# A list scheduler that is told of the port shared by VectorE and GpSimd, and other durations for five kinds of operation

## The chip, the cores and the metric

The kernel runs on one core of a Trainium2 chip. Its engines work side by side, each through its own queue in order: TensorE (PE in the profile) multiplies, VectorE (DVE) and ScalarE (ACT) do elementwise work, GpSimd (POOL) does elementwise work on SBUF alone, and SyncE (SP) issues the DMAs. An instruction waits for semaphores of other engines, and everything queued behind it on its engine waits too. The metric is the time in microseconds of one execution; the median of several is compared.

## The reference, cut to what matters

One decoder layer over 2048 tokens of width 1024, all in fp32:

```python
h = rmsnorm(x, norm1_g); p = h @ w_in            # 1024 -> 2560
a = pool_mixer(p[pool columns])                  # trailing means over 2, 4, 8, 16 tokens
b = diff_attention(q, k, v, lam)                 # 4 heads: (softmax(q1 k1) - lam softmax(q2 k2)) v, causal
c = stick_breaking_attention(q, k, v)            # 4 heads: sigmoid scores times a running product, causal
x = x + concat(a, b, c) @ w_out
h2 = rmsnorm(x, norm2_g)
x = x + (silu(h2 @ w_gate) * (h2 @ w_up)) @ w_down   # 1024 -> 2816 -> 1024
return rmsnorm(x, final_norm_g)
```

## The kernel before, in words

**Numbers.** Each fp32 operand of a large product is held as two parts, a high part (ScalarE, `split`, L415) and the remainder (VectorE, L416); a product is three matmuls (L474 to L476, L562 to L564, L914 to L916): high by high, high by low, low by high.

**Stages.** The tokens go in four tiles of 512. The input projection of a tile (`a1_tile`: RMSNorm, transposes L462, drains L465 and L467, products L474 to L476 and L562 to L564) stores q, k and v to DRAM. Attention takes a tile pair by pair. Four pairs are differential (`att_diff`): scores L648/L649 with a mask L651, maximum on DVE L717, exponential on ACT L720, softmax statistics of one column on DVE L729 to L757, a scaling on POOL L742, the mix of the two maps on DVE L763. Two pairs are stick-breaking (`att_sb`): sigmoids on ACT L796 and L798, a scan on DVE L806, a product on POOL L810. Both then transpose (L672), split (L415, L416) and multiply by v (L771 to L773, L816 and L817). The output projection (`out_proj`) reads the heads back (L412), scales them (L882/L883 on PE, L887 on DVE), and multiplies by w_out, L914 to L916. The projections of later and earlier tiles are the work that PE does between the attention steps.

The SwiGLU part (`mlp`) comes last. Each 2x2 block product is made of seven half-size products with sums and differences of blocks (Strassen's scheme). `gate_up` takes weight columns in 22 steps for each of two token halves (`s`): POOL forms the weight sums (`add`, L952), ACT and DVE split them, PE does seven products (L474 to L476), ACT copies a bank out (L1107), DVE adds banks (L1111), ACT applies the SiLU (L1114), DVE multiplies (L1117), POOL forms sums of the results (L952) and SP stores them (L1120). In the first half `head_out` also prepares the second half's operands: POOL subtractions L1061 on blocks read back with DMAs (L1055). `down` loads w_down, forms sums alternately on DVE and POOL (L952), splits, multiplies, and adds the banks into the result (DVE L1303); `finish` normalises and stores (ACT L437, root steps on DVE L423 to L431, L1286).

**What sets the order.** Nothing of this is ordered by hand. Every step is recorded as an `Op` with an engine, a duration in ns, a priority and the buffers that it reads and writes. `Plan.schedule` then plays the program: an engine that becomes free takes, of the steps whose inputs are there by the plan's clock, the one of smallest priority, and the engines' instructions are issued in the order of the planned starts. The order is fixed from then on; the chip follows it with semaphores. The durations come from small formulas (`act_ns`, `dve_ns`, `scan_ns`, `pool_ns`, `dma_ns`) and constants, and a hand-over costs the `LAG` of the engine. Buffers are slots of rings, and a step that needs a slot waits in the plan until one is free. The plan knows each engine as independent of the others:

```python
# Plan.schedule, before: a ready step c is taken when its buffers are there
o.start, o.end = t, t + o.ns
free[e] = o.end
```

Of the kernel before, what the change touches and what calls it, by code (L numbers as in the profile page):

```python
# [97 lines left out]
class Op:  # L98
    __slots__ = ("eng", "ns", "fn", "prio", "deps", "need", "bufs", "seq", "ready", "start", "end", "out", "plan")


class Plan:
# [4 lines left out]
    MORE = {"dma": 1080.0, "pe": 0.0}  # L107

# [6 lines left out]
    def op(self, eng, ns, fn, r=(), w=(), prio=0.0):  # L115
# [23 lines left out]
        o.deps, o.bufs, o.plan = {d for d in deps if d.plan is self}, bufs, self  # L139
        for b in bufs:  # L140
            b.users.append(o)
# [3 lines left out]
    def schedule(self):  # L145
# [31 lines left out]
        for o in self.ops:  # L177
            if o.need == 0:
                heapq.heappush(future[o.eng], (0.0, o.seq, o))
        wake = [(free[e], e) for e in self.ENGINES]  # L180
        heapq.heapify(wake)
        done = []
        while wake:
# [40 lines left out]
            free[e] = o.end  # L224
            heapq.heappush(wake, (o.end, e))
# [37 lines left out]
def scan_ns(n):  # L263
    return 2.11 * n + 70
# [6 lines left out]
def dma_ns(nbytes):  # L271
    return max(nbytes / 360.0, 450.0)
# [3 lines left out]
def hybrid_block_kernel(  # L276
# [19 lines left out]
    nc = tc.nc  # L296
# [122 lines left out]
    def rsqrt(pl, rg, v, vb, n, prio):  # L419
# [3 lines left out]
        pl.op("dve", 75, lambda: nc.vector.tensor_scalar(  # L423
            yt().bitcast(I32), v().bitcast(I32), 1, None, ALU.logical_shift_right), r=[vb], w=[y], prio=prio)
        pl.op("dve", 75, lambda: nc.vector.tensor_scalar(
            yt().bitcast(I32), yt().bitcast(I32), -1, 0x5F3759DF, ALU.mult, ALU.add), r=[], w=[y], prio=prio)
        for _ in range(3):
            pl.op("dve", 75, lambda: nc.vector.tensor_mul(zt(), yt(), yt()), r=[y], w=[z], prio=prio)
            pl.op("dve", 75, lambda: nc.vector.scalar_tensor_tensor(
                zt(), zt(), -0.5, v(), ALU.mult, ALU.mult), r=[vb], w=[z], prio=prio)  # L430
            pl.op("dve", 75, lambda: nc.vector.scalar_tensor_tensor(  # L431
# [269 lines left out]
    def att_diff(pl, rg, t, p, q, ks, vs, prio):  # L701
        pv = rg["pv"].new()
        nch = t + 1
        for qp in range(2):
            rows = []
            for qb in range(2):
# [41 lines left out]
                pl.op("dve", 190, lambda lc=lc, sm=sm: nc.vector.reciprocal(sm.t[:, 28:29], sm.t[:, lc[1]:lc[1] + 1]),  # L748
                      r=lk + [(sm, "L")], w=[(sm, "rho")], prio=prio("stat"))
                pl.op("dve", 70, lambda lc=lc, sm=sm: nc.vector.tensor_scalar(  # L750
                    sm.t[:, 28:29], sm.t[:, 28:29], sm.t[:, lc[0]:lc[0] + 1], neglam, ALU.mult, ALU.mult),
                    r=lk + [(sm, "L"), c_lam], w=[(sm, "rho")], prio=prio("stat"))
                if nch > 1:
                    pl.op("dve", 70, lambda sm=sm: nc.vector.tensor_scalar_mul(
                        sm.t[:, 32:32 + nch], sm.t[:, 20:20 + nch], sm.t[:, 28:29]),
                        r=[(sm, ("f", 1))], w=[(sm, "rho")], prio=prio("stat"))
                pl.op("dve", 70, lambda lc=lc, g=g, sm=sm: nc.vector.tensor_copy(  # L757
# [705 lines left out]
```

## Time and profile before

| | |
|---|---|
| time of three runs | 2685.91 us median (2684.29 to 2689.05) |
| the profiled execution's own time | 2685.21 us |
| its span, first to last instruction | 2683.3 us |
| PE busy | 2582.0 us, 96%, 13836 matmul records |
| DVE busy | 1768.1 us, 66% |
| ACT busy | 1323.8 us, 49% |
| POOL busy | 879.9 us, 33% |
| mean granted clock of TensorE | 0.982 of full speed |
| DMA | 436.41 MB, mean 163 GB/s |

Busy time is the union of the instructions' spans on an engine. A row of a timeline has a start, a length, the engine, line and operation, and in brackets the idle time of the engine ahead of it with what ended it. TensorE's clock has two levels, 1.00 (2.4 GHz) and 0.50 (1.2 GHz).

### The profile page before, as it was taken

Reading aid. Unit: us, or ns where it says so; the run is one execution under the profiler, and the core shown is the slowest. Engines: PE = TensorE matmul, PEld = TensorE weight load, DVE = VectorE, ACT = ScalarE, POOL = GpSimd, SP = SyncE. Lnnn points to the kernel's source line nnn. Section 1 sums busy time; section 2 is a strip of 40 time slices with the busy share of each in tenths; the row PEclk is TensorE's granted clock in tenths of the full one; section 3 lists DMA queues with packets and bytes.
Section 4 is the critical chain, followed back from the end, with each engine's and each line's share of the span. In section 5 each row is a group of like instructions: output and inputs, shape, how many; then the busy total and the mean of one; then the engine's idle time right before and its main releaser. Section 6 shows DMA issues by size and latency. Waiting matters only on the chain.

```text
span 2683.3 us, 39226 instructions
## 1 busy us (share of the span) xinstructions
PE 2582.0 (96%) x13836; PEld 2158.9 (80%) x13836; DVE 1768.1 (66%) x3127; ACT 1323.8 (49%) x2645; POOL 879.9 (33%) x890
## 2 busy tenths in 40 slices
PE   8989989999999999998899999999999999999998
PEld 6878778878888788878878887887888887888886
DVE  6376977779778888886554554475444447558557
ACT  4265666657767566664433533353333333445444
POOL 2001313222443133241024466544544444132041
PEclk9999999999999999988999999999999999999999
DMA  6776564566455845535632455253222338335333
GB/s 209 243 263 199 198 226 155 169 207 214 137 169 154 274 142 177 197 126 166 198 119 99 168 171 187 107 174 109 103 109 88 113 136 298 104 95 197 93 91 121
DMA packets 192709, 436.41 MB, mean 163 GB/s; under 512 B 21240, under 2 KB 58232, under 8 KB 192512
## 3 DMA queue, kind: packets, MB, share of 16 engines
q1 hardware_dynamic: 192512, 433.91, 48.7%
q8 instruction: 108, 1.77, 0.3%
q14 instruction: 89, 0.73, 0.1%
HBM read 313.77 MB, written 120.06 MB: 162 GB/s over the span
## 4 chain that ended last, share of the span: by engine, by line
PE 62%; DVE 9%; DMA 4%; ACT 3%; issue 2%; POOL 2%; SPq 0%; DVEq 0%; POOLq 0%; ACTq 0%
PE bank L476 15%; PE bank L474 15%; PE bank L475 15%; DVE d L416 3%; PE bank L672 3%; PE bank L648 2%; DVE d L806 2%; PE bank L649 2%; PE bank L915 2%; PE bank L914 2%; PE bank L916 2%; DMA d<-wo_d 1%; POOL d L952 1%; PE bank L817 1%; PE bank L816 1%
## 5 line engine op out<-in xcount | busy, mean ns | idle before, releaser
L474 PE MATMUL bank<-d 128*128 128x512 f32 x2296 | 916.2, 399 | 8.4 <-ACT d L415 4.2
L476 PE MATMUL bank<-d 128*128 128x512 f32 x2296 | 908.6, 396 | 6.7 <-DVE d L416 6.4
L416 DVE TENSOR_TENSOR d<-d 128x512 fp32r<-128x512 f32 (+1 forms) x668 | 608.8, 934 | 458.4 <-ACT d L415 231.7
L475 PE MATMUL bank<-d 128*128 128x512 f32 x2296 | 906.8, 395 | 3.4 <-DVE d L416 3.4
L952 POOL TENSOR_TENSOR d<-d 128x512 f32<-128x512 f32 x336 | 520.6, 1558 | 870.4 <-DVE d L416 610.2
L415 ACT CAST d<-d 128x512 fp32r<-128x512 f32 (+1 forms) x668 | 489.0, 762 | 611.4 <-PE bank L476 364.7
L476 PEld LDWEIGHTS bank<-d 128*128 128x128 f32 x2296 | 433.5, 189 | 111.5 <-DVE d L416 11.0
L474 PEld LDWEIGHTS bank<-d 128*128 128x128 f32 x2296 | 434.7, 189 | 106.6 <-ACT d L415 5.6
L475 PEld LDWEIGHTS bank<-d 128*128 128x128 f32 x2296 | 434.2, 189 | 100.8 <-DVE d L416 5.3
L416 DVE TENSOR_TENSOR d<-bank,d 128x512 fp32r<-128x512 f32 (+4 forms) x381 | 220.0, 604 | 113.6 <-ACT d L415 104.8
L810 POOL TENSOR_TENSOR d<-d 128x512 f32<-128x512 f32 (+3 forms) x160 | 164.4, 1028 | 390.2 <-DVE d L806 323.8
L415 ACT CAST d<-bank 128x512 fp32r<-128x512 f32 (+4 forms) x381 | 187.7, 527 | 184.7 <-PE bank L672 108.2
L720 ACT ACTIVATE d<-bank,d 128x512 f32<-128x512 f32 (+3 forms) x320 | 198.6, 626 | 107.1 <-DVE d L717 102.5
L742 POOL TENSOR_SCALAR d<-d 128x512 f32<-128x512 f32 (+3 forms) x144 | 102.8, 730 | 440.5 <-ACT d L732 394.6
L648 PE MATMUL bank<-d 128*128 128x512 f32 (+3 forms) x480 | 199.9, 417 | 28.8 <-ACT d L720 10.9
L1107 ACT COPY d<-bank 128x512 f32<-128x512 f32 x132 | 77.6, 588 | 257.1 <-PE bank L476 231.9
L717 DVE TENSOR_REDUCE d<-bank 128x1 f32<-128x512 f32 (+3 forms) x320 | 186.8, 602 | 25.1 <-PE bank L649 12.6
L1111 DVE TENSOR_TENSOR d<-bank,d 128x512 f32<-128x512 f32 x176 | 121.1, 688 | 124.6 <-PE bank L476 117.8
L806 DVE TENSOR_TENSOR_SCAN d<-d,bank 128x512 f32<-128x512 f32 (+3 forms) x160 | 174.4, 1091 | 33.3 <-ACT d L798 15.6
L649 PE MATMUL bank<-d 128*128 128x512 f32 (+3 forms) x480 | 176.7, 371 | 0.0
L672 PE MATMUL bank<-ident,d 128*128 128x128 f32 x1088 | 156.3, 276 | 6.5 <-DVE d L763 5.4
L914 PE MATMUL bank<-d 128*128 128x256 f32 x512 | 153.3, 299 | 3.9 <-DMA d<-wo_d 2.8
(134 smaller groups left out, 3563.4 us busy)
## 6 DMA issues: line engine op xcount, KB each, us to landing
d<-in_w_gu_dram SPq DMA_DIRECT2D x88, 512.0 KB, 3.5
d<-in_w_in_dram SPq DMA_DIRECT2D x80, 512.0 KB, 4.9
d<-v_d SPq DMA_DIRECT2D x60, 512.0 KB, 4.3
d<-k_d SPq DMA_DIRECT2D x60, 512.0 KB, 4.8
d<-wo_d SPq DMA_DIRECT2D x52, 512.0 KB, 5.3
d<-q_d SPq DMA_DIRECT2D x48, 512.0 KB, 4.5
g_d<-d SPq DMA_DIRECT2D x66, 256.0 KB, 2.1
d<-g_d SPq DMA_DIRECT2D x66, 256.0 KB, 2.7
```

The source lines that it names most:

```text
L415: pl.op("act", act_ns(n, psum), lambda: nc.scalar.copy(hi(), src()), r=r, w=[whi], prio=prio)
L416: pl.op("dve", dve_ns(n), lambda: nc.vector.tensor_sub(lo(), src(), f32(hi())), r=[*r, *after, whi], w=[wlo], prio=prio)
L474: nc.tensor.matmul(o, a_hi, b_hi, start=first, stop=False, **kw)
L475: nc.tensor.matmul(o, a_hi, b_lo, start=False, stop=False, **kw)
L476: nc.tensor.matmul(o, a_lo, b_hi, start=False, stop=last, **kw)
L648: nc.tensor.matmul(s.t[:, :n], qh.t[:, c0:c0 + P], kt.t[:, r, :n], start=True, stop=False)
L649: nc.tensor.matmul(s.t[:, :n], qh.t[:, c0 + 256:c0 + 256 + P], kt.t[:, r, :n], start=False, stop=j < t)
L672: nc.tensor.transpose(tp.t[:, c:c + P], rows[qb][kb // 4].t[:, (kb % 4) * P:(kb % 4 + 1) * P], ident)
L720: pl.op("act", act_ns(n, True, 2), lambda s=s, n=n, e=e, mc=mc, lc=lc, sm=sm: nc.scalar.activation(e.t[:, :n], s.t[:, :n], AF.Exp, bias=sm ...
L806: pl.op("dve", scan_ns(n), lambda iv=iv, n=n, w=w, s=s, prev=prev: nc.vector.tensor_tensor_scan(iv.t[:, n - 1::-1], w.t[:, n - 1::-1], s.t ...
L914: nc.tensor.matmul(o, m[:, 0, cs], wh.t[:, k % 4, :], start=k == 0, stop=False)
L952: pl.op(eng, ns, lambda: en.tensor_tensor(out(), a(), b(), op), r=r, w=w, prio=prio)
```

## The change

The planner's rules and numbers are changed; no instruction is added or removed, and the counts on each engine in the built program are the same. Four things:

1. **The port.** A step gets a mark `port` if it runs on POOL, or if it runs on DVE, touches no PSUM bank, and calls an operation with two tensor inputs. While a marked step of one of the two engines runs in the plan, a marked step of the other is put off until its end. Where both become free at the same instant, the plan looks at DVE first. The chip is told nothing of this: only the order that comes out is issued.
2. **Durations on DVE.** The scan 2.20 n + 65 ns instead of 2.11 n + 70; the steps of the reciprocal root 105 ns instead of 75; four steps of the softmax statistics 70, 185, 135 and 110 instead of 190, 70, 70 and 70.
3. **Transfers.** 330 bytes per ns instead of 360 (512 KB: 1589 ns instead of 1456).
4. `TWO` names operations by the function that the step's code calls: `tensor_sub`, `tensor_mul`, `tensor_add`, `tensor_tensor`, `scalar_tensor_tensor`; the scan, reductions, copies and `tensor_scalar` aren't marked.

```diff
+    PORT = {"dve": "pool", "pool": "dve"}
+    TWO = {"tensor_sub", "tensor_mul", "tensor_add", "tensor_tensor", "scalar_tensor_tensor"}
...
+        psum = any(isinstance(b.ring.slots[0], tuple) for b in bufs)
+        o.port = eng == "pool" or eng == "dve" and not psum and not self.TWO.isdisjoint(fn.__code__.co_names)
...
+        port = {e: -1e9 for e in self.PORT}
...
+                if c.port and port[self.PORT[e]] > t:
+                    heapq.heappush(fut, (port[self.PORT[e]], c.seq, c))
+                    continue
...
+            if o.port:
+                port[e] = o.end
...
 def scan_ns(n):
-    return 2.11 * n + 70
+    return 2.20 * n + 65
...
 def dma_ns(nbytes):
-    return max(nbytes / 360.0, 450.0)
+    return max(nbytes / 330.0, 450.0)
...
-        pl.op("dve", 75, lambda: nc.vector.tensor_scalar(
+        pl.op("dve", 105, lambda: nc.vector.tensor_scalar(
...
-                pl.op("dve", 190, lambda lc=lc, sm=sm: nc.vector.reciprocal(sm.t[:, 28:29], sm.t[:, lc[1]:lc[1] + 1]),
+                pl.op("dve", 70, lambda lc=lc, sm=sm: nc.vector.reciprocal(sm.t[:, 28:29], sm.t[:, lc[1]:lc[1] + 1]),
```

In the new file a line stands 11 further down (L952 is L963, L720 is L731). PE's own order is the same behind the last score block of attention (L648), to the end of the program, but for eight transposes (L1040) that moved behind the first twelve gate_up matmuls. Ahead of it, groups of projection matmuls changed places with attention steps. Three places where the order of other engines moved follow.

**Place 1, ACT, the first attention pair of the program** (about 140 us). L720 (new L731) is the exponential of a score block, and frees its bank; L415 (L426) splits an input weight that a DMA brings; L465 (L476) drains transposes of the next tile. Before:

```order
L720 ACTIVATE d<-bank_226,d 128x128
L415 CAST d<-d 128x1024
L465 ACTIVATE d<-bank_214,g_sb 128x512
L465 ACTIVATE d<-bank_210,g_sb 128x512
L720 ACTIVATE d<-bank_218,d 128x128
L720 ACTIVATE d<-bank_222,d 128x256
L720 ACTIVATE d<-bank_226,d 128x256
```

After:

```order
L731 ACTIVATE d<-bank_226,d 128x128
L731 ACTIVATE d<-bank_218,d 128x128
L476 ACTIVATE d<-bank_214,g_sb 128x512
L731 ACTIVATE d<-bank_222,d 128x256
L731 ACTIVATE d<-bank_226,d 128x256
L476 ACTIVATE d<-bank_210,g_sb 128x512
L476 ACTIVATE d<-bank_214,g_sb 128x512
L426 CAST d<-d 128x1024
```

The weight split and one drain moved from ahead of the second exponential to behind the fourth.

**Place 2, POOL, the second half's operands within gate_up** (about 1580 to 1640 us). L1061 (L1072) is an operand subtraction, L952 (L963) a weight sum or a sum of results. Before:

```order
L1061 TENSOR_TENSOR d<-d 128x256 x10
L952 TENSOR_TENSOR d<-d 128x512
L1061 TENSOR_TENSOR d<-d 128x256 x2
L952 TENSOR_TENSOR d<-d 128x512 x2
L1061 TENSOR_TENSOR d<-d 128x256
L952 TENSOR_TENSOR d<-d 128x512 x2
L1061 TENSOR_TENSOR d<-d 128x256
L952 TENSOR_TENSOR d<-d 128x512
L1061 TENSOR_TENSOR d<-d 128x256
L952 TENSOR_TENSOR d<-d 128x512
L1061 TENSOR_TENSOR d<-d 128x256 x5
L952 TENSOR_TENSOR d<-d 128x512
```

After:

```order
L1072 TENSOR_TENSOR d<-d 128x256 x8
L963 TENSOR_TENSOR d<-d 128x512
L1072 TENSOR_TENSOR d<-d 128x256 x2
L963 TENSOR_TENSOR d<-d 128x512 x5
L1072 TENSOR_TENSOR d<-d 128x256
L963 TENSOR_TENSOR d<-d 128x512
L1072 TENSOR_TENSOR d<-d 128x256 x5
L963 TENSOR_TENSOR d<-d 128x512 x5
L1072 TENSOR_TENSOR d<-d 128x256 x8
```

The four weight sums of a step now stand together with the sum of results, with no operand subtraction between them.

**Place 3, DVE, the first product of `down`** (about 2240 to 2277 us). L416 (L427) splits an operand of the running product, L952 (L963) forms a weight sum for the third product, L1303 (L1314) adds the first banks. Before:

```order
L416 TENSOR_TENSOR d<-d 128x512 x8
L952 TENSOR_TENSOR d<-d 128x512
L416 TENSOR_TENSOR d<-d 128x512 x2
L952 TENSOR_TENSOR d<-d 128x512
L416 TENSOR_TENSOR d<-d 128x512 x2
L952 TENSOR_TENSOR d<-d 128x512
L416 TENSOR_TENSOR d<-d 128x512 x2
L952 TENSOR_TENSOR d<-d 128x512 x2
L416 TENSOR_TENSOR d<-d 128x512 x2
L952 TENSOR_TENSOR d<-d 128x512
L416 TENSOR_TENSOR d<-d 128x512 x2
L952 TENSOR_TENSOR d<-d 128x512
```

After:

```order
L427 TENSOR_TENSOR d<-d 128x512 x10
L963 TENSOR_TENSOR d<-d 128x512
L427 TENSOR_TENSOR d<-d 128x512 x2
L963 TENSOR_TENSOR d<-d 128x512
L427 TENSOR_TENSOR d<-d 128x512 x2
L963 TENSOR_TENSOR d<-d 128x512
L427 TENSOR_TENSOR d<-d 128x512 x2
L963 TENSOR_TENSOR d<-d 128x512
L427 TENSOR_TENSOR d<-d 128x512 x2
L963 TENSOR_TENSOR d<-d 128x512
L1314 TENSOR_TENSOR d<-bank_238,d 128x512
```

Five weight sums stand ahead of the first bank addition instead of seven.

## Rows read from the trace of the kernel before

**Rows 1.** Stretches: length, busy us (instructions) by engine, granted clock, DMA share, GB/s
```profile
200.00:1240.00 1040.00, 998.79 (x6414) 862.39 (x6413) 841.82 (x1566) 679.51 (x1550) 310.70 (x488) 0.98 0.56 183
1240.00:1350.00 110.00, 94.94 (x728) 90.20 (x728) 60.19 (x133) 38.18 (x73) 6.23 (x4) 0.92 0.53 172
2300.00:2400.00 100.00, 100.00 (x432) 80.74 (x431) 57.27 (x90) 41.14 (x72) 36.12 (x22) 1.00 0.32 90
```
**Rows 2.** Timeline of DVE and POOL near 1800 us, and either alone elsewhere
```profile
1805.47 8.55 DVE L416 TENSOR_TENSOR d<-d 128x512 fp32r<-128x512 f32 x5
1802.90 14.46 POOL L952 TENSOR_TENSOR d<-d 128x512 f32<-128x512 f32 x8 [4.29 <-DVE d L416]
2271.29 1.28 DVE L416 TENSOR_TENSOR d<-d 128x512 fp32r<-128x512 f32 x2
1539.82 1.29 POOL L952 TENSOR_TENSOR d<-d 128x512 f32<-128x512 f32 x1
```
**Rows 3.** Groups by line and form: count, busy us, mean ns, idle before
```profile
L806 DVE TENSOR_TENSOR_SCAN d<-d,bank 128x512 f32<-128x512 f32 x112 | 142.0, 1268 | 21.7 <-ACT d L798 6.2 <-ACT d L796 4.5 <-POOL d L801 2.3
L748 DVE RECIPROCAL d<-d 128x1 f32<-128x1 f32 x64 | 9.9, 155 | 1.6 <-ACT d L720 0.9
L750 DVE TENSOR_SCALAR d<-d,neglam 128x1 f32<-128x1 f32 x64 | 17.1, 267 | 0.0
```
**Rows 4.** Timeline of PE and ACT near 140 us
```profile
144.59 0.44 PE L648 MATMUL bank<-d 128*128 128x384 f32 x1 [3.98 <-ACT d L720]
141.97 1.04 ACT L415 CAST d<-d 128x1024 fp32r<-128x1024 f32 x1 [2.56 <-DMA d<-in_w_in_dram]
142.92 1.26 ACT L465 ACTIVATE d<-bank,g_sb 128x512 fp32r<-128x512 f32 x2
144.07 0.37 ACT L720 ACTIVATE d<-bank,d 128x128 f32<-128x128 f32 x1
```
**Rows 5.** Stretches, same columns as group 1
```profile
145.33:148.75 3.42, 3.42 (x16) 2.48 (x16) 2.76 (x11) 0.83 (x4) 0.00 (x0) 0.50 0.81 228
1630.00:1637.00 7.00, 6.22 (x15) 4.87 (x16) 0.63 (x1) 1.42 (x4) 6.03 (x8) 0.51 0.94 299
1632.00:1636.00 4.00, 4.00 (x10) 3.10 (x10) 0.00 (x0) 0.00 (x0) 3.10 (x5) 0.50 0.94 288
1640.00:1644.00 4.00, 4.00 (x19) 3.25 (x18) 3.23 (x5) 1.76 (x3) 2.56 (x2) 1.00 0.93 269
```
**Rows 6.** Timeline of POOL, ACT and PE, 1618 to 1631 us
```profile
1622.36 0.74 POOL L1061 TENSOR_TENSOR d<-d 128x256 f32<-128x256 f32 x1 [2.60 <-DMA d<-h_d]
1625.44 1.29 POOL L952 TENSOR_TENSOR d<-d 128x512 f32<-128x512 f32 x1
1628.68 1.04 ACT L415 CAST d<-d 128x1024 fp32r<-128x1024 f32 x1 [8.61 <-POOL d L952]
1630.78 0.80 PE L474 MATMUL bank<-d 128*128 128x512 f32 x1 [3.05 <-ACT d L1107]
```
**Rows 7.** Timeline of DVE from 2257 us; who waited for whom on PE, 2250 to 2280
```profile
2257.42 1.36 DVE L952 TENSOR_TENSOR d<-d 128x512 f32<-128x512 f32 x1 [0.33 <-DMA d<-in_w_down_dram]
2266.08 3.48 DVE L952 TENSOR_TENSOR d<-d 128x512 f32<-128x512 f32 x2
...
PE bank L476 <- DVE d L416: 3.1, 3, 1.2
PE bank L475 <- DVE d L416: 2.3, 3, 1.2
```
**Rows 8.** Timeline of PE near 2661 us, 1816 us, 1258 us and 401 us
```profile
2662.64 0.50 PE L475 MATMUL bank<-d 128*128 128x512 f32 x1 [1.06 <-DVE d L416]
1816.28 0.79 PE L476 MATMUL bank<-d 128*128 128x512 f32 x1 [2.63 <-DVE d L416]
1258.22 0.79 PE L882 MATMUL bank<-d,sel 8*128 8x512 f32 x1 [7.52 <-DVE d L887]
401.24 0.45 PE L648 MATMUL bank<-d 128*128 128x128 f32 x1 [4.66 <-DMA d<-k_d]
```

More of the change, by code (lines that the diff above doesn't have):

```diff
@@ L98 @@
 class Op:
-    __slots__ = ("eng", "ns", "fn", "prio", "deps", "need", "bufs", "seq", "ready", "start", "end", "out", "plan")
+    __slots__ = ("eng", "ns", "fn", "prio", "deps", "need", "bufs", "seq", "ready", "start", "end", "out", "plan", "port")
 class Plan:
@@ L422, in rsqrt @@
         yt, zt = (lambda: y.t[:, :n]), (lambda: z.t[:, :n])
-        pl.op("dve", 75, lambda: nc.vector.tensor_scalar(
+        pl.op("dve", 105, lambda: nc.vector.tensor_scalar(
             yt().bitcast(I32), v().bitcast(I32), 1, None, ALU.logical_shift_right), r=[vb], w=[y], prio=prio)
-        pl.op("dve", 75, lambda: nc.vector.tensor_scalar(
+        pl.op("dve", 105, lambda: nc.vector.tensor_scalar(
             yt().bitcast(I32), yt().bitcast(I32), -1, 0x5F3759DF, ALU.mult, ALU.add), r=[], w=[y], prio=prio)
         for _ in range(3):
-            pl.op("dve", 75, lambda: nc.vector.tensor_mul(zt(), yt(), yt()), r=[y], w=[z], prio=prio)
-            pl.op("dve", 75, lambda: nc.vector.scalar_tensor_tensor(
+            pl.op("dve", 105, lambda: nc.vector.tensor_mul(zt(), yt(), yt()), r=[y], w=[z], prio=prio)
+            pl.op("dve", 105, lambda: nc.vector.scalar_tensor_tensor(
                 zt(), zt(), -0.5, v(), ALU.mult, ALU.mult), r=[vb], w=[z], prio=prio)
-            pl.op("dve", 75, lambda: nc.vector.scalar_tensor_tensor(
+            pl.op("dve", 105, lambda: nc.vector.scalar_tensor_tensor(
                 yt(), zt(), 1.5, yt(), ALU.add, ALU.mult), r=[z], w=[y], prio=prio)
@@ L747, in att_diff @@
                     lk.append((sm, "L"))
-                pl.op("dve", 190, lambda lc=lc, sm=sm: nc.vector.reciprocal(sm.t[:, 28:29], sm.t[:, lc[1]:lc[1] + 1]),
+                pl.op("dve", 70, lambda lc=lc, sm=sm: nc.vector.reciprocal(sm.t[:, 28:29], sm.t[:, lc[1]:lc[1] + 1]),
                       r=lk + [(sm, "L")], w=[(sm, "rho")], prio=prio("stat"))
-                pl.op("dve", 70, lambda lc=lc, sm=sm: nc.vector.tensor_scalar(
+                pl.op("dve", 185, lambda lc=lc, sm=sm: nc.vector.tensor_scalar(
                     sm.t[:, 28:29], sm.t[:, 28:29], sm.t[:, lc[0]:lc[0] + 1], neglam, ALU.mult, ALU.mult),
@@ L753, in att_diff @@
                 if nch > 1:
-                    pl.op("dve", 70, lambda sm=sm: nc.vector.tensor_scalar_mul(
+                    pl.op("dve", 135, lambda sm=sm: nc.vector.tensor_scalar_mul(
                         sm.t[:, 32:32 + nch], sm.t[:, 20:20 + nch], sm.t[:, 28:29]),
                         r=[(sm, ("f", 1))], w=[(sm, "rho")], prio=prio("stat"))
-                pl.op("dve", 70, lambda lc=lc, g=g, sm=sm: nc.vector.tensor_copy(
+                pl.op("dve", 110, lambda lc=lc, g=g, sm=sm: nc.vector.tensor_copy(
                     l1[t][:, g, p:p + 1], sm.t[:, lc[0]:lc[0] + 1]),
```

## The prediction

> **What bounds the kernel now.** I read the stretches first. In the SwiGLU part PE is the bound: a full stretch of 100 us holds 432 matmuls of 512 columns, 0.2315 us each, with no idle time at all [rows 1]. That can't become shorter by another order; only the few places where PE stands still there can. From 200 to 1240 us, attention with projections between its steps, PE's records cover 998.8 of 1040 us, so 41.2 us are idle, DVE's cover 841.8 (81%) [rows 1]. From 1240 to 1350 us PE has 15.1 us idle. So what an order can win is the sum of PE's stops, and I went through PE's waits in order of time, then looked on the engine that ended each for what stood ahead of the releasing instruction.
>
> A stop costs more than its gap, since the granted clock fell to 0.50 (1.2 GHz) behind the first two of the stops below, after idle PE. Its price is read at either level: 10 matmul records in 4 us at 0.50, 19 at 1.00 [rows 5], so a half-clock stretch loses 9/19 of its length. The 7 us window at a mean of 0.51 holds 2 x 0.49 x 7 = 6.9 us of it, worth 3.2 us; the 3.42 us one is worth 1.6 us.
>
> **What the change tells the planner, against the trace.** No instruction is added or removed, so the direct price is nothing; all of it is what order comes out. The port rule is what the rows show: near 1805 us five splits of DVE took 8.55 us, 1.71 us each, while POOL's eight sums took 14.46 us, 1.81 us each; apart, two splits took 1.28 us and one sum 1.29 us [rows 2]. They took turns. The scan's 1268 ns record is nearer to the new 1191 than to the old 1150, the reciprocal's 155 ns is nearer to 70 than 190, the step behind it at 267 ns nearer to 185 than 70 [rows 3]. The planner's clock comes closer to the chip's, and most where DVE and POOL share the port, in the SwiGLU part, and where an instruction waits for a transfer.
>
> **Place 1, 140 us.** PE stood 3.98 us for an exponential, L720. On ACT a weight split L415 had come first, which itself waited 2.56 us for its DMA, then two drains L465 of 1.26 us; the L720 ran at 144.07 [rows 4]. With transfers counted longer, the split stands behind the fourth exponential. The gap's 3.98 us and the clock's 1.6 us could go, 5.6 us in all. But the first drain now waits for one exponential more and the others for three, some 0.4 to 1.3 us by L720's 0.37 us and larger forms, and transposes need those banks. I take 4.0; the bounds are 0 (the split's wait for the DMA just stops the next exponentials) and 5.6.
>
> **Place 2, 1631 us.** PE stood 3.05 us for a bank copy L1107 of ACT. The copy stood behind a split L415 that had waited 8.61 us for POOL's sum L952, and that sum stood behind operand subtractions L1061, one of which idled POOL for 2.60 us on a DMA of h_d [rows 6]. The old plan slipped a subtraction between sums that depend on each other; the new one issues five sums in a row. A sum can't be held up by h_d in the middle of its step then. Gap and clock are 3.05 + 3.2 = 6.3 us. I take 6.0; the bounds are 0 (eight subtractions in a row stand ahead of the sums, and an idle wait in them holds up the sums as before) and 6.3. What is late next there is the bank addition on DVE, which waits for PE there and not for POOL, so I cost it at nothing.
>
> **Place 3, 2254 to 2277 us.** PE waited six times for splits, 3.1 + 2.3 = 5.4 us [rows 7], without a fall of the clock. DVE had seven sums L952 between the splits of the first product; with POOL's turns they took 1.36 us, or 3.48 us for two [rows 7]. Two of the seven move behind the first bank additions, where the second product has its splits early. At some 1.4 us each, that is 2.8 us. The bounds are 0 and 5.4.
>
> **Place 4, 2661 us.** PE stood 1.06 us for a split [rows 8] that came behind two of the last normalisations L1286 on DVE. In the new order the last of these splits stand ahead of both. I take 1.0. The tail behind the last matmul has the same links, so nothing more.
>
> **Place 5, against it, 1816 us.** PE stood 2.63 us for the end of the run of five splits in [rows 2, 8]. The new order has six splits of that form in the run, between the same multiplication L1117 and bank addition L1111. POOL's sums are still there. One more split at 1.71 us: +1.7, bounds 0 and 1.7.
>
> **Unchanged.** At 1258 us PE stood 7.52 us for a head that had to be scaled; the four loads of heads are queued on SP behind the same loads of x, and both orders are equal there. At 401 us it stood 4.66 us for a key tile that goes to DRAM and back [rows 8]; PE's transposes ahead of it stand in the same places. I cost both at nothing.
>
> **The rest of attention.** Counting columns ahead of each score block in both orders, at 0.2315 us per 512 columns, at most 9.3 us more projection work stands ahead of the same attention step, and at most 6.4 us less. The plan puts more filler where DVE and POOL are now counted slower. That can turn some of the 41.2 us idle into work, or delay the scores that DVE waits for. I take 0 with bounds of 9.3 us either way, since at no step does more change places. On SP, single loads and stores changed places with the next one there; their landing is part of the same bounds.
>
> The Trainium skill, in SBUF — State Buffer, section "Who interferes with whom", has a rule that bears on this: whichever of the two engines issues first keeps the shared pair for its whole instruction, and issue order decides who is held up. The turns in [rows 2] agree. By that rule a plan that looks at DVE first in a tie binds nobody on the chip, which is the second rival below.
>
> **The sum.** -4.0 - 6.0 - 2.8 - 1.0 + 1.7 + 0 = -12.1 us. Against the profiled execution's own 2685.2 us that is 2673.1; it lies 0.7 us under the median of the three runs, so I say 2673 us, 0.5% less.
>
> **The rivals.** *The stops only move* (no change): the port is shared as before whatever the plan thinks, so the places that hang on POOL's turns, 2 and 3, keep their stops, at other instructions. Left are places 1, 4 and 5: -4.0 - 1.0 + 1.7 = -3.3, so 2682 us; a band of 2680 to 2690 belongs to it. For it speaks that POOL's waits are bound to DVE's splits, whose number is the same; against it that place 2 hangs on a DMA that stands ahead of a sum, which the order does decide.
>
> *DVE starves in attention* (slower): the plan now holds POOL back whenever DVE has a marked step, so it plans the products L810 and scalings L742 later than they happen, and puts projection matmuls ahead of the next scores. DVE has then nothing to do where it is the busiest but PE, and at the end of the stage there is no filler left. The price is the 9.3 us shift, and one more half-clock stretch like the one at 1631 us (3.2 us) for each stop of 3 us; with two of these and place 5, and places 1 to 4 at half (6.9 us), that is 9.3 + 6.4 + 1.7 - 6.9 = +10.5, 2696 us. It decides from the point where PE's idle time between 200 and 1240 us grows by more than the 12 us of the forecast, to 53 us. Against it: DVE has 19% idle in that stretch, and the filler's total is the same.
>
> *Attention gains too*: the shift fills idle time, -9.3 - 12.1, so 2664 us.
>
> **How the numbers follow.** Forecast 2673 us (2667 to 2679): 0.44. Attention gains too: 0.16. Stops only move, 2680 to 2690: 0.24. DVE starves: 0.16. About 0.2%, 5.4 us, is what a measurement of this kernel can tell from no change. The first two give faster, 0.60; the third 0.24 no change; the last 0.16 slower. With all bounds in favour, -5.6 - 6.3 - 5.4 - 1.1 + 0 - 9.3, the time is 2657; the upper end has to take in part of the slower case. The range is 2657 to 2693 us.
>
> **What would show it.** Place 1: no gap of more than 1 us ahead of a score block near 140 us, and no 0.50 there. Place 2: no POOL idle time for h_d directly ahead of a sum that ACT waits for, and no half clock between 1620 and 1640 us. Place 3: PE's waits for L416 at the start of `down` under 3 us. Place 4: none near the end. Place 5: a stop of 2.6 to 4.5 us there. The port's turns should be as before, sums of POOL near 1.8 us beside DVE's splits [rows 2]. Idle PE in attention of more than 53 us would show the starving case; the prediction is wrong too if a new stop with a fall of the clock appears in the SwiGLU part, where the changed orders of ACT and DVE have places that I didn't go through.

## The result, and the profile after

The changed kernel takes 2653.26 us (median of four runs, 2647.58 to 2655.8) against 2687.16 (2684.29 to 2689.05) for the kernel before beside it: 0.9872 of the time, 95% interval 0.9852 to 0.9892, some 34 us less. The forecast was 2673 us, 12 us less, and the range began at 2657. The sign was right; the size was not. Each kernel's time is the median of its runs, without one run of f1 (6400.74 us) and one of the kernel before (4891.44 us) that stand far outside the others.

The changed file's lines are 11 further down: L415 is now L426, L416 L427, L720 L731, L887 L898, L952 L963, L1061 L1072. First the stretches of [rows 1] and the two parts into which everything below is divided: the **attention part**, up to PE's last product of the output projection, and the **SwiGLU part**, from there to the last matmul. In these rows come the stretch in us, its length, then busy time and number of records of PE, PEld, DVE, ACT and POOL, the mean granted clock, DMA share and GB/s. After:

```profile
200.00:1240.00 1040.00, 1005.64 (x6489) 876.92 (x6486) 843.48 (x1612) 686.17 (x1563) 310.87 (x488) 0.97 0.56 186
1240.00:1350.00 110.00, 95.10 (x678) 90.49 (x679) 55.10 (x103) 38.99 (x75) 6.32 (x4) 0.87 0.52 171
1350.00:2650.00 1300.00, 1288.55 (x5572) 1043.31 (x5570) 738.36 (x1135) 504.49 (x819) 540.82 (x364) 1.00 0.40 135
...
0.00:1339.00 1339.00, 1277.38 (x8237) 1118.19 (x8238) 1001.38 (x1976) 811.49 (x1810) 333.11 (x526) 0.96 0.58 192
1339.00:2641.00 1302.00, 1295.93 (x5600) 1049.06 (x5599) 739.70 (x1121) 511.13 (x834) 542.57 (x365) 1.00 0.41 136
```

And the attention part of the kernel before, as one stretch:

```profile
0.00:1349.00 1349.00, 1276.69 (x8233) 1107.08 (x8234) 1014.18 (x1977) 812.13 (x1811) 334.63 (x526) 0.97 0.58 190
```

The same 8235 or so matmuls end at 1339 us instead of 1349. By the end of PE's last record of L916 the attention part went from 1349.5 to 1339.0 us, **10.6 us less**; the SwiGLU part went from 1323.2 to 1302.3 us, **20.9 us less**; the tail behind the last matmul gave 1.2 back. The span is 30.3 us shorter in these two executions. In the SwiGLU part PE's order is the same in both but for the eight transposes at its start; PE has 6.1 us idle left of 18.5, and half clock (0.50, 1.2 GHz) for 6.8 us instead of 20.5.

PE's stops that answer to [rows 4, 6, 8], after (start, length, engine, line, operation, shapes, in brackets the idle time ahead and what ended it):

```profile
60.64 0.77 PE L485 MATMUL bank<-d,bdh 128*128 128x512 f32 x1 [3.80 <-DVE d L427]
152.39 0.79 PE L659 MATMUL bank<-d 128*128 128x512 f32 x1 [2.70 <-ACT d L731]
395.66 0.45 PE L659 MATMUL bank<-d 128*128 128x128 f32 x1 [1.26 <-DMA d<-k_d]
1244.42 0.79 PE L893 MATMUL bank<-d,sel 8*128 8x512 f32 x1 [7.03 <-DVE d L898]
1795.06 0.50 PE L485 MATMUL bank<-d 128*128 128x512 f32 x1 [1.40 <-ACT d L426]
```

The stop at 1631 us of [rows 6] is gone; the place is now at 1615 us. So is the one at 2661. The stop at 1816 us [rows 8] shrank from 2.63 us to 0.53, with the 1.40 ahead of it that the last row shows. Place 1 still stops, 2.70 us for an exponential where it was 3.98, and a stop of 3.80 us at 57 us is new; the same matmul had waited 0.53 us before:

```profile
57.54 0.47 PE L474 MATMUL bank<-d,bdh 128*128 128x512 f32 x1 [0.53 <-ACT d L415]
```

PE's SwiGLU instructions stand in one order in every kernel here, but for eight transposes L1040 at the start, which stand behind twelve gate_up matmuls in the change, f9, f10, f12 and g3. So the time at PE's n-th matmul can be compared directly. Between the end of the attention part and matmul 9019 the change gains 1.4 us, from there past place 2 (to 9460) 6.7, past place 5 (to 10356) 3.0, to 12086 0.8, through place 3 (to 12150) 7.0, to the end, with place 4, 2.0. That is the 20.9. The 3.0 of place 5 is a sum: the 240 matmuls around its stop give 2.8, a stop of 0.82 us for a bank copy at 1855 us that went gives 1.1, and the matmuls ahead, with a new stop of 0.35 us at 1755 us, take 0.7 back.

### The profile page after: what moved, and what is told of

Read it like the earlier page. It is cut to its first block, busy times and chain, and to the rows that moved or that the text cites. A ratio compares the mean times of both kernels' runs of the same rounds, so it can differ in the third digit from the quotient of the medians.

```text
span 2653.0 us, 39234 instructions
## 1 busy us (share of the span) xinstructions
PE 2573.6 (97%) x13836; PEld 2167.2 (82%) x13836; DVE 1749.4 (66%) x3127; ACT 1323.8 (50%) x2645; POOL 875.7 (33%) x890
## 4 chain that ended last, share of the span: by engine, by line
PE 82%; DVE 7%; DMA 5%; ACT 3%; issue 2%; SPq 0%; POOL 0%; DVEq 0%; ACTq 0%; POOLq 0%
PE bank L485 18%; PE bank L487 18%; PE bank L486 18%; PE bank L683 4%; PE bank L659 4%; PE bank L660 3%; DVE d L427 3%; PE bank L926 2%; PE bank L925 2%; PE bank L927 2%; PE bank L573 2%; PE bank L574 2%; PE bank L575 2%; PE bank L828 1%; PE bank L827 1%
## 5 line engine op out<-in xcount | busy, mean ns | idle before, releaser
L427 DVE TENSOR_TENSOR d<-d 128x512 fp32r<-128x512 f32 (+1 forms) x668 | 601.8, 923 | 434.9 <-ACT d L426 223.0
L963 POOL TENSOR_TENSOR d<-d 128x512 f32<-128x512 f32 x336 | 520.1, 1556 | 854.8 <-DVE d L427 629.5
L426 ACT CAST d<-d 128x512 fp32r<-128x512 f32 (+1 forms) x668 | 488.1, 762 | 543.5 <-PE bank L487 358.3
L427 DVE TENSOR_TENSOR d<-bank,d 128x512 fp32r<-128x512 f32 (+3 forms) x381 | 219.7, 605 | 124.4 <-ACT d L426 122.3
L426 ACT CAST d<-bank 128x512 fp32r<-128x512 f32 (+3 forms) x381 | 187.4, 528 | 196.5 <-PE bank L683 123.6
L731 ACT ACTIVATE d<-bank,d 128x512 f32<-128x512 f32 (+3 forms) x320 | 198.9, 626 | 97.5 <-DVE d L728 84.1
```

Of the source, the lines that this page charges most:

```text
L426: pl.op("act", act_ns(n, psum), lambda: nc.scalar.copy(hi(), src()), r=r, w=[whi], prio=prio)
L427: pl.op("dve", dve_ns(n), lambda: nc.vector.tensor_sub(lo(), src(), f32(hi())), r=[*r, *after, whi], w=[wlo], prio=prio)
L731: pl.op("act", act_ns(n, True, 2), lambda s=s, n=n, e=e, mc=mc, lc=lc, sm=sm: nc.scalar.activation(e.t[:, :n], s.t[:, :n], AF.Exp, bias=sm ...
L963: pl.op(eng, ns, lambda: en.tensor_tensor(out(), a(), b(), op), r=r, w=w, prio=prio)
```

## The experiments

Two parts, two questions. For the SwiGLU part: **theory A**, the port rule makes the gain, against **rival B**, the slower transfers do. For the attention part: **theory D**, a plan with truer numbers gains, against **theory S**, any other order lands by chance within some 10 us (later 25) of before. A **theory E**, on the stop of 7 us at the end of attention, comes up with f9 and is named in some expectations ahead of it: the stop comes when more products of the output projection are left behind the last score block than stand behind the request for the last heads.

### One part of the change at a time

f1 has only the port rule, f2 only the durations on DVE, f3 only the transfers:

```diff
 # f1, against the changed kernel: the old scan_ns, root steps, statistics and
-    return max(nbytes / 330.0, 450.0)
+    return max(nbytes / 360.0, 450.0)
 # f2: the old transfers and
-                if c.port and port[self.PORT[e]] > t:
+                if False and c.port and port[self.PORT[e]] > t:
 # f3: without the rule, with the old durations, 330 kept
```

> The kernel before with the port rule alone; all durations and the 360 bytes per ns as before. Parts of the gain of 30.3 us of span in the trace of after: 10.6 us up to the last matmul of the output projection (attention part), 20.9 us from there to the last matmul (SwiGLU part, where PE's order is the same in both). Theory A, the port rule makes the SwiGLU gain: here the SwiGLU part is 18 to 22 us shorter than before, POOL's five weight sums stand in a row and no half clock is left near 1630 us. Rival B, the slower transfers make it: here the SwiGLU part is within 6 us of before. For the attention part theory S (any other order falls by chance within some 10 us of before on either side) says anything from -12 to +10; theory D (it is the plan's truer port that gains) says -8 to -14 us. Total by A with D about 2655 us.

> The kernel before with the durations of scan, root steps and softmax statistics alone, no port rule, 360 bytes per ns. POOL's order in the SwiGLU part and DVE's at the start of the last product are word for word those of before, so theories A and B both say that the SwiGLU part is within 2 us of before and keeps its stops near 1631, 1816 and 2257 us. The attention part: theory S says anything from -12 to +10 us, and theory D that it stays within 4 us of before. Total 2676 to 2698 us by S, 2682 to 2691 by D.

> The kernel before with 330 instead of 360 bytes per ns alone. Rival B, the slower transfers make the SwiGLU gain: 15 to 22 us shorter from the last output projection matmul on. Theory A: 0 to 8 us shorter, since POOL's weight sums stand four in a row in one step and as before in the other, and the splits at 1816 us still meet a full run of POOL's sums. Attention part: theory S from -12 to +10 us; if the plan's transfers make the attention gain, -8 to -14 us and the stop for the key tile near 401 us (4.66 us before, 1.26 us after) is gone here.

(The labels are shortened to f1, f2 and so on.) Measured: f1 2647.0 us, ratio 0.9856 (0.9829 to 0.9882); f2 2663.31, 0.9924 (0.9902 to 0.9945); f3 2677.32, 0.9969 (0.9955 to 0.9982). SwiGLU part: f1 20.1 us shorter, f2 0.8, f3 2.2. Theory A stands and B falls. (f3's profiled execution is one of its slowest: its two parts give 3.4 us where the medians differ by 8.3, so some 5 us more may belong to either part; B wanted 15 in the SwiGLU part.) In f2, PE's stops of [rows 6, 8] are where they were, and so are the rows that cause them: POOL idle for h_d in the middle of the sums, five splits at 1.71 us. f2, timelines of PE, POOL and DVE:

```profile
1607.90 0.79 PE L485 MATMUL bank<-d 128*128 128x512 f32 x1 [3.19 <-ACT d L1118]
1792.39 0.80 PE L487 MATMUL bank<-d 128*128 128x512 f32 x1 [2.63 <-DVE d L427]
...
1599.49 0.74 POOL L1072 TENSOR_TENSOR d<-d 128x256 f32<-128x256 f32 x1 [2.88 <-DMA d<-h_d]
1606.41 2.49 POOL L963 TENSOR_TENSOR d<-d 128x512 f32<-128x512 f32 x2
...
1781.56 8.56 DVE L427 TENSOR_TENSOR d<-d 128x512 fp32r<-128x512 f32 x5
```

The attention part was the surprise: f1 23.3 us shorter, f2 22.2, f3 1.2. Theory D had f1 at 8 to 14 us shorter and f2 within 4 us of before, theory S both at 12 us shorter at most.

### The rule in the SwiGLU part alone

```diff
         o.port = eng == "pool" or eng == "dve" and not psum and ...
+        o.port = o.port and fn.__code__.co_firstlineno >= 961      # f4
+        o.port = o.port and self.marking                           # f5
...
+    plan.marking = True                                            # f5
     mlp(plan, rm, 6e6)
```

> The kernel before with the port rule, where only steps recorded in the SwiGLU part carry the mark. PE's whole order is that of before, and every engine's up to the end of attention. The attention part must then be within 2 us of before (a check on how far equal orders scatter). Theory A: the SwiGLU part is 12 to 21 us shorter, less than 20.9 only where POOL's order near 1631 us, which has three sums in a row here and not five, keeps that stop (6 us). Rival B: within 6 us of before. Total by A 2666 to 2675 us, by B 2680 to 2687.

> As f4_port_in_swiglu, but every step that is recorded for the SwiGLU part is marked, the splits on DVE too, which a helper outside that part records and which f4 therefore left without the mark. PE's order is that of before throughout; POOL's five sums in a row and DVE's order at the start of the last product are those of f1_port. Theory A (the rule acts in the SwiGLU part by itself, through the turns of sums and splits): attention part within 3 us of before, SwiGLU part 17 to 22 us shorter, total 2663 to 2670 us. Rival C (the gain of f1 there hangs on what attention leaves behind): SwiGLU part within 6 us of before, total 2680 to 2688.

f4 did not do what its text says. It marked by the line on which a step's code stands, and the splits are recorded by a helper above that line, so sums and multiplications were marked and splits were not. It measured 2686.01 us, ratio 0.9997 (0.9981 to 1.0012); SwiGLU part 3.0 us shorter. Read as what it is, it says that the rule is worth next to nothing in all unless it binds the splits: place 2 alone gave 5.0 us, and other stretches took part of that back. POOL still idles for h_d between the sums there, and PE still stops, for half as long:

```profile
1623.60 0.74 POOL L1073 TENSOR_TENSOR d<-d 128x256 f32<-128x256 f32 x1 [2.63 <-DMA d<-h_d]
1624.30 1.29 POOL L964 TENSOR_TENSOR d<-d 128x512 f32<-128x512 f32 x1
...
1630.65 0.50 PE L486 MATMUL bank<-d 128*128 128x512 f32 x1 [1.46 <-ACT d L1119]
```

f5 marks the splits too: 2670.93 us, 0.9942 (0.9927 to 0.9956). Attention part 2.4 us longer, with PE's order that of before; SwiGLU part 17.2 us shorter. So the rule acts there by itself, and rival C falls. f5, timelines of POOL near place 2 and place 5 and of DVE at place 5 (lines are one further in f4 and f5):

```profile
1615.63 1.29 POOL L964 TENSOR_TENSOR d<-d 128x512 f32<-128x512 f32 x1
1618.47 6.33 POOL L964 TENSOR_TENSOR d<-d 128x512 f32<-128x512 f32 x4 [1.55 <-DVE d L428]
1624.75 6.95 POOL L1073 TENSOR_TENSOR d<-d 128x256 f32<-128x256 f32 x8
...
1802.72 10.91 POOL L964 TENSOR_TENSOR d<-d 128x512 f32<-128x512 f32 x7 [3.56 <-DMA g_d<-d]
...
1800.77 9.21 DVE L428 TENSOR_TENSOR d<-d 128x1024 fp32r<-128x1024 f32 x7
```

And what PE waited for from 2230 to 2275 us, around place 3 (us in total, times, longest):

```profile
PE bank L488 <- DVE d L428: 1.2, 1, 1.2
PE bank L487 <- DVE d L428: 0.7, 1, 0.7
```

The five sums come without a subtraction between them, and eight subtractions follow. What each place gave, in us against before, from the times of the same matmuls:

| | place 2 | place 5 | place 3 | SwiGLU part |
|---|---|---|---|---|
| change | -6.7 | -3.0 | -7.0 | -20.9 |
| f1, rule | -6.8 | -6.1 | -5.4 | -20.1 |
| f5, rule here alone | -6.8 | -6.0 | -3.9 | -17.2 |
| f4, splits unmarked | -5.0 | +1.7 | -0.6 | -3.0 |
| f2, durations | -1.3 | -0.1 | 0.0 | -0.8 |
| f3, 330 | -2.3 | +1.0 | -2.3 | -2.2 |

### Direction or chance: the attention part

```diff
 # f6, away from the trace (f11: 2.11 n + 75 and nothing else)
-    return 2.11 * n + 70
+    return 2.02 * n + 75
-        pl.op("dve", 75, lambda: nc.vector.tensor_mul(zt(), yt(), yt()), ...
+        pl.op("dve", 45, lambda: nc.vector.tensor_mul(zt(), yt(), yt()), ...
 # f12, further towards it: 2.35 n + 65, root steps 170
```

> The kernel before with the scan and the root steps moved as far from the trace as the change moved them towards it: scan 2.02 n + 75 instead of 2.11 n + 70, root steps 45 instead of 75 ns; no port rule. It moves about as many PE instructions as f2_numbers did. Theory D (durations nearer to the trace give the 22 us that f2 gained in the attention part): here the attention part is at least 3 us longer than before. Theory S (the order of before is an unlucky draw, and another order of any cause gains or loses by chance): anything from -25 to +10 us. SwiGLU part within 3 us of before by both.

> The kernel before with one number moved by 5 ns: scan 2.11 n + 75 instead of + 70. 400 of PE's instructions change places, all in attention. It shows how far an order without a direction scatters. Theory S: the attention part moves by 5 us or more either way. Theory D (the direction of the durations matters): within 4 us of before. SwiGLU part within 2 us by both; 243 products left after the last score block, so the stop of 7 us stays by E.

> The kernel before with the scan and root steps moved further in the direction of f2, to what the trace of before shows: scan 2.35 n + 65 (1268 ns at 512 columns), root steps 170 ns; softmax statistics as in the change. No port rule, 360 bytes per ns. Theory D: the attention part is 22 to 32 us shorter than before, at least as much as in f2. Theory S: anywhere from -25 to +10 us. If f2 gained because its plan happened to end attention well (E alone), no more than the stop's 8 to 12 us is gained: 220 products are left after the last score block, as 218 in f2. SwiGLU part within 3 us of before.

f6: 2685.38 us, ratio 1.0 (0.999 to 1.001), attention part 1.3 us shorter. f11: 2686.99, 1.0005 (0.9995 to 1.0014), 2.6 us longer. f12: 2687.5, 1.0006 (0.9989 to 1.0023), 7.0 us shorter, and its SwiGLU part 10.4 us longer; root steps counted at 170 ns change DVE's order there too. Theory D as I had put it falls with f12: numbers nearer to single records of the trace gave a third of f2's gain there and nothing in all. But f6 lost time on the way (its last score block comes 22.6 us later than before) and got it back behind that, where it has less work left and no stop of 7 us. And f11, with 400 of PE's instructions moved, stays within 3 us. So S, any order good for 10 us either way, isn't what these show either.

### The parts in company

f7 is the change with 360, f8 without the rule, f10 with the old durations.

> The changed kernel with the old 360 bytes per ns: port rule and all durations. f1 (port) gained 23.3 us in the attention part, f2 (durations) 22.2, f3 (330) 1.2, all three together 10.6. If the parts have each a gain of their own and 330 loses 10 us or more in company (theory D), the attention part is 25 us or more shorter than before here, total under 2640. By S it lies anywhere between -25 and +10 with no tie to the sum of the two. SwiGLU part 18 to 22 us shorter by theory A.

> The changed kernel without the port rule: durations and 330 bytes per ns. By D with a 330 that costs nothing by itself (f3) the attention part is 20 to 24 us shorter; by D with a 330 that spoils the others 5 to 12 us; by S anywhere from -25 to +10. SwiGLU part within 5 us of before by theory A, total 2660 to 2690.

> The changed kernel with the old durations: port rule and 330 bytes per ns. 247 products are left after the last score block here, as in the changed kernel, against 197 with the port rule alone. Theory E: the stop of some 7 us with its half clock is back, and the attention part gains 10 to 16 us on before, 8 to 12 us less than f1's 23.3. If 330 adds nothing in company, as in f8 against f2, and the stop has another cause: 21 to 25 us. SwiGLU part 17 to 22 us shorter by theory A. Total 2650 to 2657 by E, 2640 to 2645 otherwise.

f7: 2658.88 us, 0.9901 (0.9887 to 0.9916), attention 10.5 us shorter, SwiGLU 18.4. f8: 2656.21, 0.9891 (0.9876 to 0.9906), 22.4 and 4.6. f10: 2663.9, 0.9918 (0.9901 to 0.9935), 7.9 and 14.4. The SwiGLU part is 14.4 us or more shorter wherever the rule binds the splits, and at most 4.6 us shorter where it doesn't. The attention gains do not add up: the rule 23, the durations 22, both together 10.5. That doesn't hang on one execution: the medians, less the SwiGLU part, give some 18 and 24 us for the rule (f1, g2), 22 for the durations and 9 for both. So D, with 25 us or more for f7, missed there; f8 fell below its range of totals, and f10 missed what E had for it (10 to 16 us of attention, 2650 to 2657 us) and what A had for its SwiGLU part (17 to 22).

### The stop of 7 us at the end of attention

Before and changed kernel have 244 and 247 output products of PE behind the last score block, and 205 behind the request for the last tile's heads, counted in the program's order; f1 has 197 and 202, so attention steps still run beside the request, and its stop is 1.22 us. f9 requests the heads one quarter earlier:

```diff
-AHEAD = 2
+AHEAD = 1
```

> The changed kernel with AHEAD 1 instead of 2: the heads of the last tile are requested one quarter of the output projection of tile 2 earlier. Only 79 of PE's 13974 instructions change places, all around the end of attention; 236 products of the output projection stand behind the request instead of 205, with 247 behind the last score block in both. Theory E: the 7 us stop near 1237 us and the half-clock stretch of 13.7 us at it come from the chain request, load, scaling, split, which has neither score blocks nor products to cover it when more products than those behind the request are left after the last score block (before and after: 244 and 247 against 205; f1: 197 against 202). Then the stop falls under 2 us here and the attention part is 7 to 13 us shorter than in the changed kernel, total 2640 to 2647 us. Rival F: the head loads wait on SP behind a load of x that waits for a store; then the stop stays over 5 us and the time within 3 us of 2653.

2652.04 us, 0.9877 (0.9858 to 0.9896): the same as the change. The stop did go, and two others stand where PE now meets the last attention pair without cover:

```profile
1227.28 1.87 PE L702 MATMUL bank<-ones_c,d 128*128 128x2 f32 x8 [2.49 <-ACT d L696]
1230.97 0.79 PE L893 MATMUL bank<-d,sel 8*128 8x512 f32 x1 [1.83 <-DVE d L898]
```

F is out, since the stop moved with the request and not with SP's queue; E named its cause and overrated its price. f10, with 247 products left, has the stop back at 6.88 us, as E said, though not the total.

### Again, and put together

g2 is f1, g3 the change, a second time on one chip; g1 has the durations everywhere and the rule in the SwiGLU part alone.

> The durations of the change everywhere, the port rule for steps recorded for the SwiGLU part alone (splits too), 360 bytes per ns. PE's order is that of f2_numbers to the last instruction, POOL's order in the SwiGLU part that of f1_port. If the two parts are separate: attention part 19 to 25 us shorter as in f2, SwiGLU part 15 to 21 us shorter as in f5, total 2643 to 2652 us, 35 us or more under before. If what one part gains is given back in the other: over 2655 us.

> f1_port a second time. If the attention part's 23 us belong to the order: 19 to 27 us again. If they were the scatter of one execution: nearer to 10. The total 3 to 10 us under the changed kernel in the first case, within 3 us in the second.

> The changed kernel a second time, on the chip of g1 and g2. If its attention part's 10.6 us belong to the order (with the stop of 7 us near 1237 us): 7 to 14 us shorter than before again, and the total 3 to 10 us over g2; if they were scatter: anything up to 20 us.

g1: 2649.02 us, 0.9848 (0.9831 to 0.9865); g2: 2646.4, 0.9842 (0.9823 to 0.9861); g3: 2655.15, 0.9872 (0.9855 to 0.9889). In g1 the attention part is 21.4 us shorter (f2: 22.2) and the SwiGLU part 18.6 (f5: 17.2): the two parts are separate and add up. g3 repeats the change: 14.8 and 19.1. g2's profiled execution, at 2653.55 us the slowest of its four, has only 11.9 in attention where f1 had 23.3, with one program; f1's profiled execution was its fastest. Rows of f1 and of g2 over the attention part:

```profile
0.00:1326.00 1326.00, 1268.19 (x8236) 1107.91 (x8236) 1004.47 (x1977) 809.88 (x1810) 335.81 (x526) 0.98 0.60 194
...
0.00:1337.00 1337.00, 1276.15 (x8233) 1116.21 (x8234) 1003.60 (x1977) 810.04 (x1810) 335.10 (x526) 0.97 0.58 192
```

Idle PE time hardly differs, 57.8 and 60.9 us; PE is busy 8 us longer with the same matmuls, at half clock for 78.5 us instead of 58.0. So one execution's attention part is good to some 10 us. By that part g2 speaks for scatter, by its total for the order; the medians say more: the rule alone stands 6 and 9 us under the change in the two studies. Their intervals overlap, so I don't call it faster, only not slower.

g1 and f7 differ in one thing, whether the rule binds the attention part too: 0.9848 (0.9831 to 0.9865) without, 0.9901 (0.9887 to 0.9916) with it, 21.4 against 10.5 us of attention. With the old durations the rule gains there (f1 against f5); with the new ones it loses some 11 us.

## Why the prediction missed, point by point

**What bounds the kernel** was read rightly: the time moved by PE's stops and the half clock behind them. In the SwiGLU part the idle time fell by 12.4 us, and 13.7 us less at half clock are worth 6.5 by the prediction's 9/19, 18.9 of the 20.9. In the attention part the idle time fell by 10.7 us and PE's busy time stayed.

**The steps that failed** are three terms of the sum. The rest of attention was put at nothing and gave 13.8 us; place 5 had the wrong sign, 4.7 us off; place 3 was charged for two sums alone, 4.2 us short. A stop that no term had, at 57 us, took 4.8 back. From the two profiled executions (us):

| term | taken | measured |
|---|---|---|
| place 1 | -4.0 | -1.5 |
| new stop at 57 us | none | +4.8 |
| rest of attention, with 401 and 1258 us | 0 | -13.8 |
| place 2 | -6.0 | -6.7 |
| place 5, its stretch | +1.7 | -3.0 |
| place 3 | -2.8 | -7.0 |
| place 4, its stretch | -1.0 | -2.0 |
| other SwiGLU stretches | 0 | -2.2 |
| tail | 0 | +1.2 |
| sum | -12.1 | -30.3 |

**Place 1** (-4.0, bounds 0 and -5.6): mis-sized. From the first score block, the same matmul of PE in every kernel, the tile's transposes take 16.8 us before and 15.2 after. It is the transfers' number that moved them: 14.6 to 15.2 us in the six kernels with 330 (the change, f3, f8, f9, f10, g3), 16.0 to 18.4 in all others. But most of the stop stayed, and 3.4 us of half clock with it. The lower bound had named why: the split's wait for its DMA stops the next exponentials. ACT, after:

```profile
149.57 1.04 ACT L426 CAST d<-d 128x1024 fp32r<-128x1024 f32 x1 [1.37 <-DMA d<-in_w_in_dram]
150.52 1.26 ACT L476 ACTIVATE d<-bank,g_sb 128x512 fp32r<-128x512 f32 x2
151.67 0.58 ACT L731 ACTIVATE d<-bank,d 128x384 f32<-128x384 f32 x1
```

The same three links stand there as in [rows 4], four exponentials further on.

**The stop at 57 us** (no term): the rule lets wide weight splits on DVE come ahead of the one that PE waits for. 3.80 us of idle time and 6.8 us of half clock behind it make the first score block start 4.8 us later, so that the transposes of place 1 end 3.3 us later in the trace although place 1 gained. Before, then after:

```profile
138.19 0.22 PE L648 MATMUL bank<-d 128*128 128x128 f32 x1
143.00 0.22 PE L659 MATMUL bank<-d 128*128 128x128 f32 x1
```

The stop is in every kernel with the rule in the input projection (f1, f7, f9, f10, g2, g3) and in none without.

**Place 2** (-6.0): right in size and cause. It measured -6.7. The stretch around the place, after:

```profile
1600.00:1625.00 25.00, 25.00 (x110) 20.21 (x109) 16.48 (x17) 7.99 (x12) 21.24 (x20) 1.00 0.72 226
```

PE has no idle time in that stretch. POOL's timeline in it:

```profile
1597.71 4.76 POOL L1072 TENSOR_TENSOR d<-d 128x256 f32<-128x256 f32 x5
1602.43 8.64 POOL L963 TENSOR_TENSOR d<-d 128x512 f32<-128x512 f32 x5
1611.04 6.95 POOL L1072 TENSOR_TENSOR d<-d 128x256 f32<-128x256 f32 x8
```

The five sums run without a subtraction among them, and none of them waits.

**Place 3** (-2.8, bounds 0 and -5.4): mis-sized. It measured -7.0. I had charged two sums of the seven at 1.4 us each. But the rest got cheaper too: the seven sums had taken 9.76 us, two of them one behind the other 3.48 [rows 7]; the five that are left take 4.67. One still takes 1.78 us, but the last two 0.68, as short as the shortest of before. DVE after, its five sums:

```profile
2228.37 0.69 DVE L963 TENSOR_TENSOR d<-d 128x512 f32<-128x512 f32 x1 [0.42 <-DMA d<-in_w_down_dram]
2232.46 0.84 DVE L963 TENSOR_TENSOR d<-d 128x512 f32<-128x512 f32 x1 [0.86 <-DMA d<-in_w_down_dram]
2236.63 1.78 DVE L963 TENSOR_TENSOR d<-d 128x512 f32<-128x512 f32 x1
2240.64 0.68 DVE L963 TENSOR_TENSOR d<-d 128x512 f32<-128x512 f32 x1
2243.55 0.68 DVE L963 TENSOR_TENSOR d<-d 128x512 f32<-128x512 f32 x1
```

What PE waited for from 2202 to 2277 us, where [rows 7] has 3.1 and 2.3 us, and the two stretches at the place:

```profile
PE bank L487 <- DVE d L427: 0.3, 1, 0.3
```

```profile
2227.00:2242.00 15.00, 15.00 (x66) 12.20 (x65) 13.32 (x13) 5.87 (x11) 10.60 (x7) 1.00 0.85 290
2242.00:2257.00 15.00, 15.00 (x66) 12.18 (x65) 15.00 (x22) 6.23 (x11) 9.44 (x5) 1.00 0.91 304
```

PE's idle time between these 64 matmuls, 5.6 us with the short gaps, is gone. The other 1.4 us are busy time, beyond the bound: the matmul behind each of the six stops had a record of some 0.50 us where a full stretch has one matmul every 0.23. One of them, before:

```profile
2262.21 0.50 PE L476 MATMUL bank<-d 128*128 128x512 f32 x1 [1.17 <-DVE d L416]
```

Both parts of the change had a share: the rule alone gave 5.4 us here, the transfers alone 2.3.

**Place 4** (-1.0): the 1.06 us stop is gone; the stretch from place 3 to the end gave 2.0.

**Place 5** (+1.7): the wrong sign, -3.0 in its stretch and -2.8 around the stop. I added a sixth split at the 1.71 us that each of five had taken, as if POOL's sums would run beside all of them again. They don't: POOL's run ends after four sums, and the splits behind it are alone.

```profile
1784.70 8.10 DVE L427 TENSOR_TENSOR d<-d 128x512 fp32r<-128x512 f32 x6
1784.92 6.73 POOL L963 TENSOR_TENSOR d<-d 128x512 f32<-128x512 f32 x4 [1.83 <-DVE d L1128]
```

Six take 8.10 us, 1.35 each, less than five did [rows 2]; four sums of 1.68 and two splits of 0.64 make 8.0. The clock had fallen behind this stop too, which the prediction had not priced, and half clock is 3.4 us there now instead of 6.8. Before:

```profile
1814.00:1821.00 7.00, 4.72 (x11) 3.76 (x12) 4.44 (x5) 2.72 (x5) 3.36 (x2) 0.53 0.44 150
```

The mean of POOL's 336 sums is as before, 1556 ns against 1558: turns are still taken, elsewhere. The Trainium skill, SBUF — State Buffer, section "Who interferes with whom", says that issue order decides who is held up. These rows agree as far as they go, 8.10 us for six splits against 8.55 for five with what stands beside them; they don't show which of two instructions issued first. The rival "The stops only move" (the first of the prediction's list, which calls it the second) is answered by the places: the port is shared as much as before, and the stops there went.

**Unchanged** at 1258 us held (7.03 for 7.52 us). At 401 us it did not: 1.26 for 4.66, in a place where PE's own order was equal, which had been my reason to put it at nothing.

**The rest of attention** (0, bounds 9.3 either way): the bound failed. I had counted how much projection work changes places, but a stop depends on what stands there, and PE had 67 us of them. The change gained 13.8 us here, f1 and f2 more than 20. PE's idle time in the attention part by what ended it (us, gaps over 60 ns from 30 us on, one execution each, lines of before):

| ended by | before | change | f1 rule | f2 durations | f3 330 | f6 away | f11 5 ns |
|---|---|---|---|---|---|---|---|
| key tile k_d, DMA | 6.6 | 1.3 | 2.8 | 1.4 | 1.1 | 8.0 | 5.8 |
| mix L763, DVE | 5.5 | 1.1 | 1.6 | 2.2 | 4.1 | 3.6 | 5.2 |
| scan L806 and softmax sum L737, DVE | 10.1 | 3.4 | 6.8 | 7.9 | 7.5 | 9.1 | 7.8 |
| head scaling L887, DVE | 7.9 | 10.0 | 1.6 | 2.9 | 10.0 | 2.0 | 8.2 |
| exponential L720, ACT | 11.4 | 13.4 | 8.6 | 12.1 | 7.5 | 12.3 | 14.1 |
| all | 67.1 | 56.6 | 53.0 | 53.7 | 65.4 | 64.2 | 65.0 |
| attention part | | -10.6 | -23.3 | -22.2 | -1.2 | -1.3 | +2.6 |

The change shed most of the waits for the key tile, the mix and the scan, and kept those for the heads; the rule alone and the durations alone shed the waits for the heads too. The sums fall where the attention part does, except in f11, which is 17 us longer at half clock; in f1 and f2 the part falls further, and they are 14 and 17 us less at half clock. But half clock has no fixed price here: the change has 37.5 us more of it in this part, 17.8 us by the prediction's 9/19, and PE's busy time hardly moved (1277.38 us after, 1276.69 before). What stays **open** is why: the gains don't add, numbers still nearer to the trace lose most of them (f12), the rule gains with the old durations and loses with the new (f1, g1, f7), and the one stop that I could move alone (f9) gave nothing. It wasn't settled whether the order of before is a poor draw or whether the rule and the durations help for a reason.

**The rival that starves DVE** didn't come: PE's idle time from 200 to 1240 us fell from 41.2 to 34.4 us. "Attention gains too" was the case nearest to what happened, with 16% given to it.

## What to carry to other kernels

Where a scheduler's plan sets the order, tell it of a shared resource, and mark every kind of step that holds the resource: in the SwiGLU part the rule was worth 3 us with the splits unmarked, and 14 to 20 with them (f1, f5, f7, f10, g1). Then test it part by part and with the durations that will stand beside it, since in the attention part it gained with one set of them and lost with the other. When you cost such a change, don't carry a contended duration (1.71 us a split) into the new order: look there for what runs beside each instruction. And give the part of a program in which stops of all kinds take turns a range as wide as those stops, not as the work that moves; the range of 9.3 us was too narrow for a part with 67 us of them.

## What the runs showed that I had not expected

The rule alone does as well as the whole change or better: 2647.0 and 2646.4 us against 2653.26 and 2655.15. The rule in the SwiGLU part with the durations, g1, gives 2649.02.

One program's attention part differed by 11 us between two executions (f1 and g2), with idle times 3 us apart and 20 us more at half clock. In the change half clock takes 109.2 us of the attention part in both profiled executions, against 71.7 before, and the part is still shorter: more time at 1.2 GHz is no proof of a slower order.
